# A decoder layer on one core: the relative bias written from the weights' queue, and a last norm that ends in columns

## The chip, the cores and the metric

The kernel runs on one NeuronCore of one Trainium2 chip. The metric is device time in microseconds (us) of one execution. TensorE is called PE in the profile, VectorE DVE, ScalarE ACT, GpSimd POOL and SyncE SP. SP and ACT each have a queue of DMA transfers of their own.

## The reference, cut to what matters

One layer: attention with a relative bias on 256 tokens of width 1024, a norm, a mixture of 32 experts of which each token takes 4, and a second norm. With 256 tokens there is one block of keys, so attention is plain causal attention.

```python
qkv = x @ w_in                                  # (256, 1024) @ (1024, 3072)
s = q k^T * Dh**-0.5 + rel_bias[t5_bucket(qpos - kpos)]   # causal, softmax, 8 heads
t = softmax(s) v @ w_out
h = layer_norm(ALPHA * x + t, ln_g[0], ln_b[0])
logits = h @ w_router + b_router                # top 4 of 32, softmax over the 4
for each chosen expert e:                       # clamped SwiGLU
    a = h @ w_gu[e] + b_gu[e];  g, u = split(a)
    f += gate * ((min(g,7) * sigmoid(1.702 g) * (clip(u,-7,7) + 1)) @ w_dn[e] + b_dn[e])
out = layer_norm(ALPHA * h + f, ln_g[1], ln_b[1])
```

## The kernel before

Everything is written out in one fixed order for each engine. Weights stream from HBM through 13 slots of 16 KB per partition (2 MB each). `fetch` takes the next slot's transfer from the list `todo`; its argument is the number of pieces, not of slots. `prefetch` issues as many as there are free slots. All weights go through the queue of SP, in the order of `todo`: six blocks of `w_in`, two slots of `w_out`, then for each expert four slots of `w_gu` and two of `w_dn`. The last expert's `w_dn` comes in another layout (`w_dl`), as four transfers of 1 MB.

**Start (L243 to L285).** SP loads the transposed input `xT` and the first block of weights (called w0 below) in pieces: four of 256 KB (L252), then two of 512 KB (L142), then the second block (w1) in two of 1 MB. ACT's queue loads the 32x8 table of the relative bias and a one-hot matrix. PE warms up on ones (L259) and multiplies the two (L269); DVE copies the product to `rrow` (L270). ACT's queue then writes `rrow` to a small DRAM tile `rd` in two transfers (L279, L280: 127 rows, then 256 rows, of 32 bytes each), and SP's queue reads it back as one overlapping pattern into `BT_rows` (L281), which must wait for both writes. Only behind that does SP issue the third block (`fetch(2)` at L282).

**Projection.** Inputs and weights are split into a high and a low part: ACT rounds the high part (`act_copy`, CAST in the profile at L180), DVE subtracts (L169 for weights, L276 for `xT`). PE then makes three products for each 128 rows of depth (L313 to L315), 96 products of 256 columns for each block of 512 columns of q and k. The block is evacuated at L323. The bias `BT` is first read by the softmax of head 0 (L362), which is issued together with the sixth of the twelve half-blocks.

**Experts.** Two experts share a gather and a scatter. `stage1` (L672) multiplies by `w_gu`, `swiglu` follows, `stage2` (L700) multiplies by `w_dn`. The loop ends with the first product of expert 30; behind it stand, in this order on PE: the transposes of its activation, a scatter, `spread_gain` (16 matmuls against the identity that copy gain and shift of the last norm to all partitions, evacuated by ACT into `gb2`), `stage1` of expert 31, `stage2` of expert 30 in two halves (one per slot of `w_dn`), and `stage2_columns` for expert 31 by column blocks (0, 1), (2) and (3), each followed by `add_columns`, which adds to `acc` and takes the norm's statistics.

**Last norm (`second_norm`).** For each of the two row tiles: aggregate (L197), square root on ACT (L198), reciprocal and one Newton step (L204 to L207), all on 128x1. The lower 512 columns are then normalized, scaled and shifted on DVE with two operations of 512 columns (L977, L978); the upper 512 are normalized on ACT (L984), scaled on POOL (L985) and shifted on DVE (L989). Four transfers of 256 KB write rows of the output. A branch follows, over further blocks for experts with more than 64 tokens; in the profiled execution it is not taken.

Of the kernel before, what the change touches and what calls it, by code (L numbers as in the profile page):

```python
# [11 lines left out]
F32 = mybir.dt.float32  # L12
# [4 lines left out]
AF = mybir.ActivationFunctionType  # L17
OP = mybir.AluOpType
# [4 lines left out]
S, D, H, DH = 256, 1024, 8, 128  # L23
NE, TOPK = 32, 4
KT = D // 128
# [3 lines left out]
EPS = 1e-5  # L29
# [31 lines left out]
def tile_decoder_layer(ctx: ExitStack, tc, a, out):  # L61
    nc = tc.nc
# [6 lines left out]
    def bank(name):  # L69
        return pm.tile([128, 512], F32, name=name)  # L70
# [5 lines left out]
    def tp_tile():  # L76
        return bank(next(three))
# [4 lines left out]
    def small(name, w, p=128, dt=F32):  # L82
        return cst.tile([p, w], dt, name=name)

    c = small("c", C_W)
# [5 lines left out]
    eps = small("eps", 1)  # L91
    ident = c[:, C_ID:C_ID + 128]
# [3 lines left out]
    gbT = c[:, C_LN:C_LN + 4 * KT]  # L96
# [5 lines left out]
    def slot(name, dt=F32):  # L102
        used[0] += 1
        assert used[0] <= W_SLOTS
        return wp.tile([128, SLOT], dt, name=name, tag="w")
# [8 lines left out]
    def source(key):  # L114
        kind, e, k = key
        if kind == "in":
            return a["w_in"][e]
        if kind == "dl":
            return a["w_dl"][k]
        return a["w_out"][k] if kind == "out" else a["w_gu" if kind == "gu" else "w_dn"][e, k]  # L120
# [10 lines left out]
    def fetch(pieces=1):  # L131
        key = todo.pop()
        src = source(key)
        t = slot("w").rearrange("p (k c) -> p k c", k=src.shape[1])
        load(t, src, pieces)
        w_tiles[key] = t

    def load(t, src, pieces):
        k = src.shape[1]
        for i in range(pieces):  # L140
            ks = slice(i * k // pieces, (i + 1) * k // pieces)
            nc.sync.dma_start(t[:, ks], src[:, ks])  # L142

    def prefetch():
        while todo and W_SLOTS - used[0] > reserve[0]:
            fetch(2 if todo[-1][0] == "dl" else 1)
# [38 lines left out]
    class Stats:  # L185
# [23 lines left out]
        def normal(self, r, engine):  # L209
            for s in HALVES:  # L210
                engine.tensor_scalar(r[:, s], r[:, s], self.mean, self.rstd, op0=OP.subtract, op1=OP.mult)
# [12 lines left out]
    x, acc = (t.rearrange("p (t d) -> p t d", t=2) for t in (BT, xT))  # L224
# [5 lines left out]
    BT_rows, BT = BT, BT.rearrange("p (s h) -> p s h", h=H)  # L230
# [4 lines left out]
    rrow = hp.tile([128, 3, H], F32, name="rrow")  # L235
# [28 lines left out]
    def rel_rows(row, ap):  # L264
        return bass.AP(tensor=rd.tensor, offset=rd.offset + row * H, ap=ap)
# [3 lines left out]
        nc.tensor.matmul(pr[:, i * H:(i + 1) * H], oh[:, i * 128:(i + 1) * 128], rb, start=True, stop=True)  # L269
    nc.vector.tensor_copy(rrow[:, :2], pr[:, :2 * H].rearrange("p (i h) -> p i h", i=2))  # L270
    fetch(2)

    def split_x(s):
        xhf, xlf = (t.rearrange("p k s -> p (k s)") for t in (xh, xl))
        act_copy(xhf[:, s], xT[:, s])
        nc.vector.tensor_tensor(xlf[:, s], xT[:, s], xhf[:, s].bitcast(F32), op=OP.subtract)  # L276

    split_x(slice(0, 256))
    nc.scalar.dma_start(rel_rows(0, [[H, 127], [1, H]]), rrow[:127, 2])  # L279
    nc.scalar.dma_start(rel_rows(127, [[H, 128], [128 * H, 2], [1, H]]), rrow[:, :2])  # L280
    nc.sync.dma_start(BT_rows, rel_rows(0, [[H, 128], [1, S * H]]))  # L281
    fetch(2)  # L282
    split(("in", ORDER[0], 0), act_copy, 4, lambda i: split_x(slice(256 << i, 512 << i)) if i < 2 else None)
    split_x(slice(1024, 2048))
    split(("in", ORDER[0], 1), act_copy, 4)  # L285
# [111 lines left out]
    for n in range(12):  # L397
        blk, i = ORDER[n // 2], n % 2
        last = n == 11
        if not last:  # L400
            split_next(("in", blk, i))
        if n == 1:
            nc.sync.dma_start(c, a["consts"])
            nc.sync.dma_start(router.rearrange("p k e -> p (k e)"), a["router"])
            reserve[0] = 1
            prefetch()
        for hh in score_at.get(n - 1, []):
            softmax(hh)
        if last:
            for hh in score_at.get(n - 1, []):  # L410
                softmax_norm(hh)
            split_next(("in", blk, i))
        (proj_qk if blk < 4 else proj_v)(blk, i)
        if i == 1:
            evac(blk, QT if blk < 2 else KTt)
        if not last:
            for hh in score_at.get(n - 1, []):
                softmax_norm(hh)
        for hh in score_at.get(n, []):
            scores(hh)  # L420
        for hh in trans_at.get(n, []):
            p_transpose(hh)
# [11 lines left out]
    stats = [Stats(hp, f"a{t}", 2 + t) for t in range(2)]  # L434
# [205 lines left out]
    mp = ctx.enter_context(tc.tile_pool(name="mp", bufs=1, reuse_waits="tile"))  # L640
# [104 lines left out]
    def spread(ps, cols, i, stop=True):  # L745

        for k in range(4):
            l = gbT[:, cols + 4 * i + k:cols + 4 * i + k + 1].to_broadcast([128, 128])
            nc.tensor.matmul(ps[:, k * 128:(k + 1) * 128], l, ident, start=True, stop=stop)
# [36 lines left out]
        nc.vector.tensor_copy(n_i, om[:, 95:96])  # L786
        nc.vector.tensor_tensor(om, om, fl, op=OP.mult)

    def spread_gain():

        for i in range(4):
            ps = tp_tile()
            spread(ps, 2 * KT, i)
            nc.scalar.copy(gb2[:, i * 512:(i + 1) * 512], ps)

    def more_blocks():

        bufs = itertools.cycle([slot("lw") for _ in range(2)])
# [125 lines left out]


    tail = slot("tail")
    gb2, aT_even = tail[:, :2 * D], tail[:, 2 * D:2 * D + 512].rearrange("p (j s c) -> p j s c", j=4, s=2)
    act_T(act, aT_even)
    pair_scatter(GT, Y, 1, False, (1,))
    GT = pair_slots_T(Gd)  # L930
    spread_gain()
    e = NE - 1
    hgu = stage1_bias(sel[:, e:e + 1].to_broadcast([3 * NE, CAP]))
    stage1(lambda k: xg[:, k, CAP:], lambda k: take(("gu", e, k)), hgu, lambda k: done(("gu", e, k)))
# [11 lines left out]
    stats = [Stats(mp, f"b{t}", 6) for t in range(2)]  # L946
# [20 lines left out]
    add_columns((2,), ("tp2", "yp"))  # L967
    stage2_columns(aT, (3,), ("hg", "hu"))
    add_columns((3,), ("o0", "o1"))
    g2, b2 = gb2[:, :D], gb2[:, D:]  # L970
    lo, hi = HALVES
    y = slot("y")[:, :2 * D].rearrange("p (t d) -> p t d", t=2)

    def scaled(st, t):

        d = y[:, t, lo]
        nc.vector.scalar_tensor_tensor(d, acc[:, t, lo], st.mean, g2[:, lo], op0=OP.subtract, op1=OP.mult)  # L977
        nc.vector.scalar_tensor_tensor(d, d, st.rstd, b2[:, lo], op0=OP.mult, op1=OP.add)  # L978
        nc.sync.dma_start(out[t * 128:(t + 1) * 128, lo], d)

    def normal(st, t):
        d = y[:, t, hi]
        nc.vector.scalar_tensor_tensor(st.v, st.mean, -1.0, st.rstd, op0=OP.mult, op1=OP.mult)
        nc.scalar.activation(d, acc[:, t, hi], AF.Identity, scale=st.rstd, bias=st.v)  # L984
        nc.gpsimd.tensor_tensor(d, d, g2[:, hi], op=OP.mult)  # L985

    def shifted(t):
        d = y[:, t, hi]
        nc.vector.tensor_tensor(d, d, b2[:, hi], op=OP.add)  # L989
        nc.sync.dma_start(out[t * 128:(t + 1) * 128, hi], d)  # L990

    def second_norm(stats):
        for st in stats:
            st.root()
        for t in range(2):
            stats[t].finish()
            normal(stats[t], t)
        for t in range(2):
            scaled(stats[t], t)
        for t in range(2):  # L1000
            shifted(t)

    second_norm(stats)
    more_blocks()
# [41 lines left out]
```

## Time and profile before

| | |
|---|---|
| median of 3 runs | 1062.68 us (1062.18 to 1062.95) |
| the profiled execution | 1062.37 us |
| its span, first to last instruction | 1060.5 us |
| PE busy | 972.7 us, 92% of the span |
| DVE, ACT, POOL busy | 272.9, 178.2, 7.3 us |
| read from HBM | 423.91 MB, 401 GB/s over the span |

The profiled execution's own time is 1.9 us longer than its span. A busy PE is not a PE at its peak: matmuls overlap and their ends are modelled. What bounds a stage is read from the chain of waits and from stretches of time. The granted clock of PE is 1.00 at the upper of its two levels (2.4 GHz) and 0.50 at the lower (1.2 GHz).

### The profile page before, as it was taken

Reading aid. Unit: us, or ns where it says so; the run is one execution under the profiler, and the core shown is the slowest. Engines: PE = TensorE matmul, PEld = TensorE weight load, DVE = VectorE, ACT = ScalarE, POOL = GpSimd, SP = SyncE. Lnnn points to the kernel's source line nnn. Section 1 sums busy time; section 2 is a strip of 40 time slices with the busy share of each in tenths; the row PEclk is TensorE's granted clock in tenths of the full one; section 3 lists DMA queues with packets and bytes.
Section 4 is the critical chain, followed back from the end, with each engine's and each line's share of the span. In section 5 each row is a group of like instructions: output and inputs, shape, how many; then the busy total and the mean of one; then the engine's idle time right before and its main releaser. Section 6 shows DMA issues by size and latency. Waiting matters only on the chain.

```text
span 1060.5 us, 11683 instructions
## 1 busy us (share of the span) xinstructions
PE 972.7 (92%) x5004; PEld 457.1 (43%) x5004; DVE 272.9 (26%) x571; ACT 178.2 (17%) x343; POOL 7.3 (1%) x8
## 2 busy tenths in 40 slices
PE   5999999999999999888888899999988898888893
PEld 5998753343434343333323353434323333333343
DVE  3467641212121212121111232221111212121115
ACT  3356241010101110101001010101001010101121
POOL 0000100000000000000000000000000000000001
PEclk7999999999999999999999989999999999999997
DMA  8993979999999999999999999999999999999991
GB/s 301 430 394 132 345 323 428 426 431 425 426 430 427 428 427 427 428 426 429 427 427 429 411 427 426 428 428 427 428 428 426 429 427 426 429 428 426 429 405 64
DMA packets 32551, 425.77 MB, mean 401 GB/s; under 512 B 4048, under 2 KB 4464, under 8 KB 6288
## 3 DMA queue, kind: packets, MB, share of 16 engines
q1 hardware_dynamic: 31728, 423.89, 95.0%
q10 hardware_dynamic: 768, 1.09, 0.3%
q8 instruction: 41, 0.67, 0.3%
q14 instruction: 14, 0.11, 0.0%
HBM read 423.91 MB, written 1.06 MB: 401 GB/s over the span
## 4 chain that ended last, share of the span: by engine, by line
DMA 60%; PE 34%; DVE 4%; ACT 2%; SPq 0%; issue 0%; DVEq 0%; ACTq 0%
DMA w<-in_w_gu 44%; DMA w<-in_w_dn 15%; PE yp L700 7%; PE hg L672 6%; PE hu L672 6%; PE tp L658 1%; PE o L742 1%; DMA w<-in_w_in 1%; PE tp L742 1%; PE tp L315 1%; PE tp L314 1%; PE tp L313 1%; PE o L313 1%; PE o L315 1%; PE o L314 1%; PE hg L715 0%
## 5 line engine op out<-in xcount | busy, mean ns | idle before, releaser
L672 PE MATMUL hg<-w,QT_KTt 128*64 128x512 f32 x960 | 249.8, 597 | 54.4 <-DMA w<-in_w_gu 54.4
L672 PE MATMUL hu<-w,QT_KTt 128*64 128x512 f32 x960 | 247.7, 592 | 0.0
L700 PE MATMUL yp<-w,QT_KTt 128*64 128x512 f32 x960 | 214.3, 599 | 0.7 <-ACT QT_KTt L690 0.7
L679 DVE TENSOR_SCALAR QT_KTt<-hg 128x512 f32<-128x512 f32 x32 | 22.1, 691 | 650.7 <-PE hg L672 650.7
L672 PEld LDWEIGHTS hg<-w,QT_KTt 128*64 128x64 f32 x960 | 65.9, 136 | 193.5 <-issue 125.9
L672 PEld LDWEIGHTS hu<-w,QT_KTt 128*64 128x64 f32 x960 | 70.8, 137 | 135.2 <-issue 135.2
L700 PEld LDWEIGHTS yp<-w,QT_KTt 128*64 128x64 f32 x960 | 66.6, 137 | 134.6 <-issue 121.2
L680 ACT ACTIVATE QT_KTt<-QT_KTt 128x512 f32<-128x512 f32 x32 | 20.1, 629 | 470.4 <-DVE QT_KTt L679 470.4
L704 ACT COPY QT_KTt<-yp 64x512 f32<-64x512 f32 x62 | 35.9, 579 | 224.4 <-PE yp L700 224.0
L658 PEld LDWEIGHTS tp<-OH,BT_xT 128*128 128x128 f32 x480 | 58.9, 200 | 12.0 <-issue 11.2
L658 PE MATMUL tp<-OH,BT_xT 128*128 128x128 f32 x480 | 63.2, 288 | 0.0
L169 DVE TENSOR_TENSOR whl<-w,whl 128x1024 fp32r<-128x1024 f32 (+1 forms) x36 | 38.1, 1102 | 27.1 <-ACT whl L180 27.1
L180 ACT CAST whl<-w 128x1024 fp32r<-128x1024 f32 (+1 forms) x36 | 32.5, 955 | 21.2 <-DMA w<-in_w_in 10.7
L564 DVE TENSOR_SCALAR QT_KTt<-tp,c 128x128 f32<-128x128 f32 x60 | 20.5, 403 | 44.4 <-PE tp L658 44.4
L742 PE MATMUL tp<-QT_KTt 128*128 128x512 f32 x60 | 30.7, 593 | 0.0
L742 PE MATMUL o<-QT_KTt 128*128 128x512 f32 x60 | 29.8, 618 | 0.0
L566 ACT ACTIVATE QT_KTt<-tp,c 128x128 f32<-128x128 f32 x60 | 22.5, 456 | 36.4 <-PE tp L658 36.4
L690 ACT COPY QT_KTt<-tp 128x512 f32<-128x512 f32 x31 | 18.6, 601 | 40.8 <-PE tp L689 36.5
L313 PE MATMUL o<-xhl,whl 128*128 128x256 f32 x48 | 14.9, 311 | 9.7 <-ACT whl L180 9.7
L681 DVE TENSOR_SCALAR hu<-hu 128x512 f32<-128x512 f32 x32 | 22.4, 699 | 3.0 <-PE hu L672 0.2
L683 DVE SCALAR_TENSOR_TENSOR QT_KTt<-hu,QT_KTt 128x512 f32<-128x512 f32 x32 | 22.1, 691 | 1.1
L682 DVE TENSOR_TENSOR QT_KTt<-QT_KTt 128x512 f32<-128x512 f32 x32 | 21.9, 684 | 0.1
(278 smaller groups left out, 785.1 us busy)
## 6 DMA issues: line engine op xcount, KB each, us to landing
w<-in_w_gu SPq DMA_DIRECT2D x128, 2048.0 KB, 39.1
w<-in_w_dn SPq DMA_DIRECT2D x62, 2048.0 KB, 39.1
w<-in_w_in SPq DMA_DIRECT2D x3, 2048.0 KB, 21.3
w<-in_w_in SPq DMA_DIRECT2D x4, 1024.0 KB, 9.3
w<-in_w_out SPq DMA_DIRECT2D x2, 2048.0 KB, 28.3
w<-in_w_dl SPq DMA_DIRECT2D x4, 1024.0 KB, 31.8
w<-in_w_in SPq DMA_DIRECT2D x4, 256.0 KB, 5.0
w<-in_w_in SPq DMA_DIRECT2D x2, 512.0 KB, 7.5
```

The source lines that it names most:

```text
L169: nc.vector.tensor_tensor(lo[:, s], w[:, s], hi[:, s].bitcast(F32), op=OP.subtract)
L180: nc.scalar.copy(o, i)
L313: nc.tensor.matmul(o, wh[:, k, js], xh[:, kk, :], start=kk == 0, stop=False)
L566: nc.scalar.activation(o, i, AF.Identity, scale=g, bias=b)
L658: nc.tensor.matmul(ps[:, k * 128:(k + 1) * 128], h[:, t, kk * 128:(kk + 1) * 128], OH[:, t].rearrange("p s c -> p (s c)"), start=t == 0, s ...
L672: nc.tensor.matmul(hgu[i][s * 64:(s + 1) * 64], xg(k), w[:, kk, q * 512:(q + 1) * 512], start=False, stop=k == KT - 1)
L679: nc.vector.tensor_scalar(g7, hgu[0], LIMIT, None, op0=OP.min)
L681: nc.vector.tensor_scalar(u7, u7, LIMIT, -LIMIT, op0=OP.min, op1=OP.max)
L683: nc.vector.scalar_tensor_tensor(sg, u7, 1.0, g7, op0=OP.add, op1=OP.mult)
L700: nc.tensor.matmul(y_ps[s], aT[:, kk % 4, kk // 4, :], w[:, k, HALVES[s ^ swap]], start=kk == 0, stop=kk == KT - 1)
L704: nc.scalar.copy(Y[s * 64:(s + 1) * 64, s ^ swap, :], y_ps[s])
L742: nc.tensor.matmul(po, GT[:, cb, t, :], Y[:, cb, :], start=True, stop=True)
```

## The change

Two parts that have nothing to do with each other.

At the start, the two writes of `rrow` move from ACT's queue to SP's, between the second and the third block of weights. The readback moves further back on SP, behind the fourth block.

At the end, `spread_gain` goes. Both row tiles share their roots (operations on 128x2). ACT normalizes the lower and DVE the upper 512 columns of each tile into `z`, PE transposes the 16 blocks of 128x128 into four PSUM banks, ACT and DVE apply scale and shift, which are now one number per partition, while they copy each 128x256 block out of PSUM, and four transfers write the output as columns (128 x 8 x 256); the host puts the axes back. `z` lies where `gb2` lay; `yT` takes the slot of `y`.

```diff
     fetch(2)
+    nc.sync.dma_start(rel_rows(0, [[H, 127], [1, H]]), rrow[:127, 2])
+    nc.sync.dma_start(rel_rows(127, [[H, 128], [128 * H, 2], [1, H]]), rrow[:, :2])
+    fetch(2)
 ...
     split_x(slice(0, 256))
-    nc.scalar.dma_start(rel_rows(0, [[H, 127], [1, H]]), rrow[:127, 2])
-    nc.scalar.dma_start(rel_rows(127, [[H, 128], [128 * H, 2], [1, H]]), rrow[:, :2])
-    nc.sync.dma_start(BT_rows, rel_rows(0, [[H, 128], [1, S * H]]))
-    fetch(2)
 ...
         if n == 1:
             nc.sync.dma_start(c, a["consts"])
             nc.sync.dma_start(router.rearrange("p k e -> p (k e)"), a["router"])
+            fetch()
+            nc.sync.dma_start(BT_rows, rel_rows(0, [[H, 128], [1, S * H]]))
 ...
-    def spread_gain():
-
-        for i in range(4):
-            ps = tp_tile()
-            spread(ps, 2 * KT, i)
-            nc.scalar.copy(gb2[:, i * 512:(i + 1) * 512], ps)
 ...
-    spread_gain()
 ...
     def second_norm(stats):
-        for st in stats:
-            st.root()
-        for t in range(2):
-            stats[t].finish()
-            normal(stats[t], t)
-        for t in range(2):
-            scaled(stats[t], t)
-        for t in range(2):
-            shifted(t)
+        u, rstd, nm, v = (r2[:, i] for i in range(4))
+        for t, st in enumerate(stats):
+            nc.vector.bn_aggr(st.t[:, 0:2], st.st.rearrange("p a b -> p (a b)"))
+            nc.scalar.activation(rstd[:, t:t + 1], st.var, AF.Sqrt, bias=eps)
+            nc.vector.tensor_scalar(v[:, t:t + 1], st.var, EPS, None, op0=OP.add)
+        nc.vector.reciprocal(rstd, rstd)
+        nc.vector.tensor_tensor(u, rstd, rstd, op=OP.mult)
+        nc.vector.tensor_tensor(u, u, v, op=OP.mult)
+        nc.vector.tensor_scalar(u, u, -0.5, 1.5, op0=OP.mult, op1=OP.add)
+        nc.vector.tensor_tensor(rstd, rstd, u, op=OP.mult)
+        for t, st in enumerate(stats):
+            nc.vector.scalar_tensor_tensor(nm[:, t:t + 1], st.mean, -1.0, rstd[:, t:t + 1], op0=OP.mult, op1=OP.mult)
+        for t, st in enumerate(stats):
+            nc.scalar.activation(z[:, t, lo], acc[:, t, lo], AF.Identity, scale=rstd[:, t:t + 1], bias=nm[:, t:t + 1])
+            nc.vector.tensor_scalar(z[:, t, hi], acc[:, t, hi], st.mean, rstd[:, t:t + 1],
+                                    op0=OP.subtract, op1=OP.mult)
+        names = ("tp0", "tp1", "tp2", "yp")
+        ps = [bank(n).rearrange("p (k s) -> p k s", k=2) for n in names]
+        for t in range(2):
+            for k in (0, 4, 1, 5, 2, 6, 3, 7):
+                nc.tensor.transpose(ps[k // 2][:, k % 2, t * 128:(t + 1) * 128], z[:, t, k * 128:(k + 1) * 128], ident)
+        for i in range(2):
+            for k in (2 * i, 2 * i + 4, 2 * i + 1, 2 * i + 5):
+                o, p = yT[:, k], ps[k // 2][:, k % 2]
+                g, b = gbT[:, 2 * KT + k:2 * KT + k + 1], gbT[:, 3 * KT + k:3 * KT + k + 1]
+                if k < 4:
+                    nc.scalar.activation(o, p, AF.Identity, scale=g, bias=b)
+                else:
+                    nc.vector.tensor_scalar(o, p, g, b, op0=OP.mult, op1=OP.add)
+            for k in (2 * i, 2 * i + 4):
+                nc.sync.dma_start(out[:, k:k + 2], yT[:, k:k + 2])
```

How the instructions stand on the engines at the two places: first ACT at the start of the program, before (`whl` is the split weight, `xhl` the split input, `rd` the DRAM tile).

```order
L180 CAST xhl<-BT_xT 128x256
L279 DMA rd<-rrow 127x8
L280 DMA rd<-rrow 128x2x8
L180 CAST whl<-w 128x512
L180 CAST xhl<-BT_xT 128x256
```

And ACT at the same place now:

```order
L180 CAST xhl<-BT_xT 128x256
L180 CAST whl<-w 128x512
L180 CAST xhl<-BT_xT 128x256
L180 CAST whl<-w 128x512
L180 CAST xhl<-BT_xT 128x512
```

The two writes no longer stand ahead of the first cast of a weight. On SP, before, from the second half of w0 on:

```order
L142 DMA w<-in_w_in 128x1024 x2
L142 DMA w<-in_w_in 128x2048 x2
L281 DMA BT_xT<-rd 128x2048
L142 DMA w<-in_w_in 128x2048 x2
L403 DMA c<-in_consts 128x452
L404 DMA router<-in_router 128x288
L142 DMA w<-in_w_in 128x4096 x3
```

And on SP now:

```order
L142 DMA w<-in_w_in 128x1024 x2
L142 DMA w<-in_w_in 128x2048 x2
L272 DMA rd<-rrow 127x8
L273 DMA rd<-rrow 128x2x8
L142 DMA w<-in_w_in 128x2048 x2
L402 DMA c<-in_consts 128x452
L403 DMA router<-in_router 128x288
L142 DMA w<-in_w_in 128x4096
L405 DMA BT_xT<-rd 128x2048
L142 DMA w<-in_w_in 128x4096 x2
```

The writes stand ahead of the third block, and the readback, which waits for them, moved from ahead of the third block to behind the fourth.

## Rows read from the trace of the kernel before

**Rows 1.** The page: shares of the span in the chain that ended last, by line.

```profile
DMA w<-in_w_gu 44%; DMA w<-in_w_dn 15%; PE yp L700 7%; PE hg L672 6%; PE hu L672 6%; PE tp L658 1%; PE o L742 1%; DMA w<-in_w_in 1%; PE tp L742 1%; PE tp L315 1%; PE tp L314 1%; PE tp L313 1%; PE o L313 1%; PE o L315 1%; PE o L314 1%; PE hg L715 0%
```

**Rows 2.** Stretches: us, busy of PE, PEld, DVE, ACT, POOL, clock, DMA share, GB/s.

```profile
16.00:20.00 4.00, 4.00 (x20) 4.00 (x20) 4.00 (x7) 4.00 (x8) 0.00 (x0) 0.50 0.28 79
...
100.00:104.00 4.00, 4.00 (x22) 3.40 (x21) 3.08 (x5) 3.56 (x4) 0.00 (x0) 1.00 0.00 0
...
148.00:152.00 4.00, 4.00 (x20) 1.15 (x16) 2.86 (x3) 1.07 (x1) 0.00 (x0) 1.00 1.05 451
...
1050.00:1055.00 5.00, 0.00 (x0) 0.00 (x0) 4.93 (x5) 0.47 (x1) 2.52 (x2) 0.50 0.14 54
```

**Rows 3.** Timeline of the start: start, duration, instruction, idle time before and its releaser.

```profile
5.65 0.42 DVE L276 TENSOR_TENSOR xhl<-BT_xT,xhl 128x256 fp32r<-128x256 f32 x1
...
6.97 7.58 ACTq L280 DMA_DIRECT2D rd<-rrow  x1
14.59 0.62 ACT L180 CAST whl<-w 128x512 fp32r<-128x512 f32 x1 [10.71 <-DMA w<-in_w_in]
...
15.26 0.58 PE L313 MATMUL o<-xhl,whl 128*128 128x256 f32 x1 [9.74 <-ACT whl L180]
...
21.49 0.35 PE L313 MATMUL o<-xhl,whl 128*128 128x256 f32 x1
...
29.82 0.28 PE L313 MATMUL hg<-xhl,whl 128*128 128x256 f32 x1
```

**Rows 4.** First block's pieces: issues on SP, and their time from issue to landing.

```profile
1.19 0.42 SPq L252 DMA_DIRECT2D w<-in_w_in  x1
...
DMA to landing us min/median/max: 3.2/5.0/5.4
...
4.51 1.46 SPq L142 DMA_DIRECT2D w<-in_w_in  x2
...
w<-in_w_in SPq DMA_DIRECT2D x1, 512.0 KB, 8.0
```

**Rows 5.** ACT's DMA queue in 6.2 to 16 and 16 to 19 us; the readback's issue.

```profile
q10 hardware_dynamic: 22, 0.00, 0.1%
...
q10 hardware_dynamic: 378, 0.01, 7.1%
...
18.73 0.33 SPq L281 DMA_DIRECT2D BT_xT<-rd  x1
```

**Rows 6.** Timeline: first casts of the third block, first use of the bias.

```profile
33.76 2.00 ACT L180 CAST whl<-w 128x1024 fp32r<-128x1024 f32 x2 [1.48 <-DVE whl L169]
...
50.66 0.94 DVE L362 SCALAR_TENSOR_TENSOR p<-hg,BT_xT 128x128 f32<-128x128 f32 x2
```

**Rows 7.** Tail: two pieces of the chain; the last `w_dn` slot, issue and landing.

```profile
1006.88 3.57 PE tp L749 x32
...
1028.76 3.58 PE yp L700 x16
...
988.86 0.33 SPq L142 DMA_DIRECT2D w<-in_w_dn  x1
...
w<-in_w_dn SPq DMA_DIRECT2D x1, 2048.0 KB, 39.1
```

**Rows 8.** Timeline of the last norm, and a scaled copy of 128 columns (page).

```profile
1046.80 0.30 DVE L197 BATCH_NORM_AGGREGATE rs_b<-st_b 128x2 f32<-128x36 f32 x1
1047.14 0.71 ACT L198 ACTIVATE rs_b<-rs_b,eps 128x1 f32<-128x1 f32 x2 [2.93 <-DVE rs_b L197]
...
1048.25 0.21 DVE L207 TENSOR_SCALAR rs_b<-rs_b 128x1 f32<-128x1 f32 x1
...
1048.69 1.77 ACT L984 ACTIVATE y<-BT_xT,rs_b 128x512 f32<-128x512 f32 x2 [0.85 <-DVE rs_b L983]
...
1055.15 0.94 SPq L990 DMA_DIRECT2D out<-y  x2
...
L566 ACT ACTIVATE QT_KTt<-tp,c 128x128 f32<-128x128 f32 x60 | 22.5, 456 | 36.4 <-PE tp L658 36.4
```

More of the change, by code (lines that the diff above doesn't have):

```diff
@@ L926, in tile_decoder_layer @@
     tail = slot("tail")
-    gb2, aT_even = tail[:, :2 * D], tail[:, 2 * D:2 * D + 512].rearrange("p (j s c) -> p j s c", j=4, s=2)
+    y, aT_even = tail[:, :2 * D], tail[:, 2 * D:2 * D + 512].rearrange("p (j s c) -> p j s c", j=4, s=2)
     act_T(act, aT_even)
@@ L969, in tile_decoder_layer @@
     add_columns((3,), ("o0", "o1"))
-    g2, b2 = gb2[:, :D], gb2[:, D:]
     lo, hi = HALVES
[L972 to L990, printed above, removed]
-    def second_norm(stats):
-        for st in stats:
-            st.root()
-        for t in range(2):
-            stats[t].finish()
-            normal(stats[t], t)
-        for t in range(2):
-            scaled(stats[t], t)
-        for t in range(2):
-            shifted(t)
+    z, yT = y.rearrange("p (t d) -> p t d", t=2), slot("yT")[:, :2 * D].rearrange("p (k s) -> p k s", k=KT)
@@ new lines, in tile_decoder_layer @@
+    r2 = mp.tile([128, 4, 2], F32, name="r2")
+    def second_norm(stats):
+        u, rstd, nm, v = (r2[:, i] for i in range(4))
[16 more added lines that the diff above has]
+        ps = [bank(n).rearrange("p (k s) -> p k s", k=2) for n in names]
+        for t in range(2):
+            for k in (0, 4, 1, 5, 2, 6, 3, 7):
[10 more added lines that the diff above has]
+                nc.sync.dma_start(out[:, k:k + 2], yT[:, k:k + 2])
@@ L1040 @@
            for k, v in arrays.items()}
-    out = nc.dram_tensor("out_0", (S, D), F32, kind="ExternalOutput").ap()
+    out = nc.dram_tensor("out_0", (128, KT, S), F32, kind="ExternalOutput").ap()
     with tile.TileContext(nc) as tc:
@@ L1044 @@
     res = run_bass_kernel_spmd(nc, [arrays], core_ids=[0])
-    return res.results[0]["out_0"].reshape(1, S, D)
+    return np.ascontiguousarray(res.results[0]["out_0"].reshape(128, KT, S).transpose(2, 1, 0)).reshape(1, S, D)
```

## The prediction

> **What bounds the kernel now.** I read the page first. The chain that ended last is 59% transfers of expert weights [rows 1], so for most of the span the kernel waits for HBM. That doesn't mean that only bytes count. The next view is the table of stretches [rows 2]: from about 148 us on the transfers run at the rate of the whole rest (451 GB/s in 148 to 152 us), but before that they stop, to 79 GB/s in 16 to 20 us and to 0 in 100 to 104 us. In these gaps the slots are full and SP waits until compute frees one. So the moment at which the saturated stretch begins is set by the chain of compute ahead of it, and whatever moves that chain moves the end of the program by the same amount, as long as the gap at 100 us and its neighbours leave room to take it from. The other place that counts is what follows the last weights.
>
> The timeline of the start [rows 3] shows where the chain of compute begins. ACT casts the first piece of weights only at 14.59 us, and PE starts on it at 15.26 after 9.74 us of idleness. The profile puts ACT's wait down to the piece's transfer. The landings contradict that [rows 4]: the first piece was issued at 1.19 us and the quickest of the four took 3.2 us, so it lies there at about 4.4, and the last of the four at 8.5 at the latest. What ends at 14.55 is the issue of the second write of `rrow`, which stands ahead of the cast on ACT and took 7.58 us. After 15.26 PE is busy without a break (4.00 of 4.00 us in 16 to 20), at first at half its clock: the clock rises at 21.49 and the block ends at 29.82 [rows 3]. From there to the experts it is never idle for long, so this start shifts everything behind it.
>
> **The start, step by step.** With both writes gone from ACT, its first weight cast runs from 4.4 to 5.0 us. PE must first finish the two small products for the bias, whose copy and the input's low half on DVE follow; DVE's row for the low half is at 5.65 and takes 0.42 [rows 3], which puts the end of PE's own products at about 5.5. PE's first real product thus starts at 5.5 and not at 15.26: 9.8 us earlier. Three bounds on that. The first product that uses the weight's low half waits for DVE: 5.65 + 0.42 for the input and about 0.7 for the weight make 6.8; it was about 0.7 behind the first product before, so this shift is at least 9.2. On the other side, before, PE ran 6.2 us at half clock (15.26 to 21.49). If the clock rises sooner after the start, up to half of the 6.2 us is won on top, 3.1, so 12.9 at most; and the data then binds: the second piece of 512 KB was issued at about 4.5 and landed 8.0 later, 12.5 [rows 4], behind which two casts of 0.62, a subtraction of 0.7 and 12 products at 0.12 remain, 15.9 us, which is early enough. If the clock rises as late as before, relative to the first product, the shift is the 9.8 itself. I take 9.8, as nearest to the rows.
>
> What SP now does instead. The two writes go into the queue behind w1, whose transfer ends at about 16.5 us as before (in 16 to 20 us only 79 GB/s are left) [rows 2]. What the writes cost there the trace doesn't show, but it bounds it. On ACT's queue hardly anything of them moved while weights were under way (22 packets up to 16 us), and 378 of the 400 went in 16 to 19 us, all before the readback's issue at 18.73 [rows 5]. Their packets took 7.1% of 16 engines in 3 us, 3.4 us of one engine, 0.009 us a packet; at the other end, if all engines worked evenly through the 2.7 us, 0.11 us a packet. The third block's first half, 1 MB or 2.4 us, then lands at 16.5 + 2.7 + 2.4 = 21.6, plus up to 1 for the landing. It is cast at 33.76 before [rows 6], so 24.0 now, and PE needs it only when the second block is done, 29.82 + 96 x 0.12 - 9.8 = 31.5, less 2.0 for its casts: 29.5. There are some 7 us of cover. The readback stands behind the fourth block: 21.6 + 2.4 + 0.9 for the constants + 4.8 + 2.4 is 32, and the bias is first read at 50.66 - 9.8 = 40.9. Both cost nothing; if the cover of 7 us went, each further us would cost one. In exchange SP no longer stands still until 18.73.
>
> A rule of the Trainium skill speaks against just this. Its page "DMA: Bandwidth & Descriptors", section "Why a DMA increments its semaphore by 16 and not by 1", says that a transfer over 127 partitions runs on a single one of the 16 engines, and "Queues, rings and completion order" says that an engine takes its descriptors in ring order. By that, the first write puts 127 of its rows ahead of every following weight on one engine. With 0.009 us each that is 1.3 us and the sum is unchanged; with 0.11 us each the price is that of the second rival below. The first of the two sections can't be checked here, since no row tells engines apart.
>
> **The tail, step by step.** `spread_gain` took 3.57 us on PE's chain [rows 7]. Its removal isn't worth that much, for PE then runs into the weights. The last slot of `w_dn` was issued at 988.86 and landed 39.1 later, at 1027.96, and the products that read it start at 1028.76 [rows 7]. So PE can come forward by some 0.7 us there and then waits; less a small delay of the release I take 0.6. The bounds are 0.3 (as long a delay as 0.5) and the full 3.57, if the last transfers get ahead of compute.
>
> The last norm: DVE aggregates from 1046.80, the first square root starts at 1047.14 and ACT's first wide operation at 1048.69 [rows 8]. Now the roots are joint: the second one ends at 1047.85, and six small operations at about 0.2 (one of them is in the rows: 0.21) bring the first wide operation to 1049.05, 0.35 later. ACT takes 0.89 for each tile (1.77 for two), so the first tile is ready at 1049.95 and the second at 1050.85; DVE's halves run beside it. Then 16 transposes: at the lower clock, to which PE has fallen by then (0.50 in 1050 to 1055 us) [rows 2], twice the 0.11 us that a pass of 128 columns costs in `spread_gain` (3.57 for 32 passes) make 3.5 us, 1049.95 to 1053.5, with the first pair of blocks complete after nine of them, 1052.0. ACT's four copies of 256 columns come at about 0.5 each (a scaled copy of 128 takes 0.456) and end at 1054.0, DVE's beside them; SP issues the last two transfers by 1054.75. Before, SP's last issue ended at 1055.15 + 0.94 = 1056.09. The last norm comes out 1.3 us shorter, provided that what follows the last issue (4.4 us to the end of the span) stays. Bounds: a transpose may cost two passes, 3.5 us more, less what ACT's copies hide then, which makes the norm 1.5 longer; at full clock 1.0 more is saved, 2.3 in all.
>
> **The sum**, against the profiled execution's 1062.37: 9.8 + 0.6 + 1.3 = 11.7, so 1050.7; the median of the runs is 0.3 above that execution, so 1051.0.
>
> **The rivals.**
>
> 1. *The start does not move.* The profile is right and the cast waited for its weights, so the writes were in nobody's way. For it: the releaser in the row. Against it: landings of at most 5.4 us. Only the tail's 1.9 remains: 1060.8.
>
> 2. *One late engine.* The 127 rows go one after another at 0.11 us, 14 us, and all following weights wait for that engine: the third block's first half lands at 16.5 + 14 + 2.4 + 1 = 33.9, 4.4 after the need. For it: small writes did wait on ACT's queue. Against it: the engine time of their packets is a twelfth of that. 1055.4.
>
> 3. *The weights' queue is held, the other sign.* SP is stopped by the writes as ACT was, and for longer, because here the whole stream stands behind them. What decides is when the third block lands: behind 29.5 every us is lost, and behind 41.2 the 11.7 are used up. ACT's hold of 7.58 us from 7 us on, even once for each write, ends at 22 and is still covered. A hold to 45 would give 1066. Nothing in the rows reaches that far.
>
> 4. *The clock rises early, or the tail wins whole.* Start 12 instead of 9.8, or `spread_gain` 3.57, or both: 1045.5 to 1048.5. For it: PE has been busy since the warm-up when the first product comes; against it: it was also busy before and began at half clock.
>
> **How the numbers follow.** My forecast (1048.5 to 1053.5) has 0.63; rival 4 has 0.15; rival 2 and smaller losses of its kind, 1053.5 to 1060, 0.13; rival 1, 0.05; rival 3, 0.04. The range of 8 in 10 takes the forecast, most of rival 4 and the near part of rival 2: 1047.0 to 1055.0. A measurement of this kernel can tell about 0.2% (2.1 us) from no change: faster 0.91, same 0.05, slower 0.04.
>
> **What would show it.** In the profile of the changed kernel the first weight cast should stand at about 4.4 us and PE's first product at 5.5, the end of the first block near 20 and the first stretch without transfers near 100 shorter by about 10. The saturated stretch should begin about 10 us earlier. In the tail PE should wait for a slot of `w_dn` or `w_dl`. From the last aggregate to SP's last issue should be 8.0 us instead of 9.3. A third block cast later than it is needed, or a first product behind 8 us, would prove me wrong.

## The result, and the profile after

The changed kernel takes 1053.47 us (median of 4 runs, 1052.76 to 1054.74), the kernel before 1062.78 in the same series (4 runs, 1062.18 to 1062.95): ratio 0.9915, 95% interval 0.9898 to 0.9932. The forecast of 1051.0 was 2.5 too low; the time lies inside the range. The profiled execution took 1053.08 us, its span is 1051.3 (before 1060.5), so 9.2 us went.

The chain of the page, in the kernel after, beside [rows 1]:

```profile
DMA w<-in_w_gu 37%; DMA w<-in_w_dn 15%; PE yp L701 9%; PE hg L673 8%; PE hu L673 8%; PE tp L659 2%; PE o L743 1%; PE tp L743 1%; PE tp L314 1%; PE tp L313 1%; PE tp L312 1%; PE o L314 1%; PE o L312 1%; PE o L313 1%; PE tp L690 1%; DVE whl L169 1%
```

Transfers fell from 59% to 52% of it. The timeline of the start, after (columns as in [rows 3]):

```profile
4.92 0.62 ACT L180 CAST whl<-w 128x512 fp32r<-128x512 f32 x1 [1.05 <-DMA w<-in_w_in]
5.71 0.38 PE L312 MATMUL o<-xhl,whl 128*128 128x256 f32 x1
7.16 0.30 SPq L272 DMA_DIRECT2D rd<-rrow  x1
7.20 0.28 PE L312 MATMUL o<-xhl,whl 128*128 128x256 f32 x1
7.74 9.46 SPq L273 DMA_DIRECT2D rd<-rrow  x1
17.25 1.08 SPq L142 DMA_DIRECT2D w<-in_w_in  x2
18.40 0.28 PE L312 MATMUL hg<-xhl,whl 128*128 128x256 f32 x1
22.92 2.00 ACT L180 CAST whl<-w 128x1024 fp32r<-128x1024 f32 x2 [2.05 <-DMA w<-in_w_in]
```

PE's first product stands at 5.71 instead of 15.26, 9.55 earlier, and the first block ends at 18.40 instead of 29.82 [rows 3], 11.4 earlier: the products are short (0.28) from 7.20 on, 1.5 us after the first one, where before they became so only after 6.2 us. The hold has moved along with the writes: 7.58 us on ACT's queue became 9.46 on SP's, and the third block is issued only at 17.25. Its first cast waits for it until 22.92. PE needs that block 96 products of 0.12 behind the first block's end, at 29.9, so the cast has until 27.9: 5 us of cover are left.

Stretches after (columns as in [rows 2]):

```profile
16.00:20.00 4.00, 4.00 (x36) 4.00 (x35) 3.07 (x5) 2.93 (x6) 0.00 (x0) 1.00 0.53 134
88.00:92.00 4.00, 4.00 (x22) 3.37 (x21) 3.02 (x5) 3.66 (x5) 0.00 (x0) 1.00 0.00 0
116.00:120.00 4.00, 4.00 (x19) 1.61 (x18) 3.03 (x18) 0.85 (x2) 1.11 (x1) 0.71 1.00 414
120.00:124.00 4.00, 4.00 (x13) 2.09 (x12) 0.22 (x2) 0.67 (x1) 0.00 (x0) 0.50 0.98 416
124.00:128.00 4.00, 4.00 (x33) 3.73 (x33) 0.26 (x1) 0.39 (x2) 0.00 (x0) 0.93 0.38 160
1040.00:1045.00 5.00, 3.67 (x16) 3.27 (x16) 2.21 (x6) 2.64 (x5) 0.00 (x0) 0.50 0.09 34
```

The stretch without transfers at 100 us, which I had forecast to be shorter, has moved instead: 0 GB/s now stand at 88 to 92 us, so there too later weights start only when compute frees slots. New to the eye is 116 to 124 us, the routing stage (the choice of the experts and the first gather): PE's granted clock is 0.71 and then 0.50. The stretches of the same stage before:

```profile
128.00:132.00 4.00, 4.00 (x17) 1.37 (x17) 2.48 (x15) 1.46 (x2) 0.51 (x1) 0.85 0.98 412
132.00:136.00 4.00, 4.00 (x24) 3.55 (x23) 0.48 (x2) 0.06 (x1) 0.00 (x0) 0.72 1.04 442
```

And its timeline before, the first tile's choice of experts (`M`) and the first product with expert weights:

```profile
128.19 0.19 DVE L521 TENSOR_TENSOR M<-lg,rest 128x32 f32<-128x32 f32 x1
...
138.14 1.08 PE L672 MATMUL hg<-w,BT_xT 128*64 128x512 f32 x4
```

The timeline after, with four 512-column products of the first bias between the two:

```profile
116.80 0.19 DVE L522 TENSOR_TENSOR M<-lg,rest 128x32 f32<-128x32 f32 x1
117.38 1.69 PE L573 MATMUL hg<-QT_KTt,c 32*64 32x512 f32 x4
128.40 1.08 PE L673 MATMUL hg<-w,BT_xT 128*64 128x512 f32 x4
```

`M` comes 11.4 us earlier and the first expert product only 9.7: 1.65 us are lost between the two. A further 0.5 goes until expert 30's last wait for `w_gu`. Its row before:

```profile
998.72 1.08 PE L672 MATMUL hg<-w,QT_KTt 128*64 128x512 f32 x4 [1.24 <-DMA w<-in_w_gu]
```

And the same row after:

```profile
989.49 1.08 PE L673 MATMUL hg<-w,QT_KTt 128*64 128x512 f32 x4 [1.24 <-DMA w<-in_w_gu]
```

The tail after, from the timeline: PE's last waits for weights, then the last norm:

```profile
1013.96 3.65 PE L701 MATMUL yp<-w,tail 128*64 128x512 f32 x16 [1.32 <-DMA w<-in_w_dn]
1018.75 3.65 PE L701 MATMUL yp<-w,tail 128*64 128x512 f32 x16 [0.56 <-DMA w<-in_w_dn]
1036.86 0.30 DVE L971 BATCH_NORM_AGGREGATE rs_b<-st_b 128x2 f32<-128x36 f32 x1
1039.18 1.52 ACT L982 ACTIVATE tail<-BT_xT,r 128x512 f32<-128x512 f32 x2 [1.28 <-DVE r L980]
1040.05 1.33 PE L989 MATMUL tp<-c,tail 128*128 128x128 f32 x5 [4.49 <-ACT tail L982]
1042.70 1.93 ACT L995 ACTIVATE yT<-tp,c 128x256 f32<-128x256 f32 x4 [1.99 <-PE tp L989]
1043.74 1.81 SPq L999 DMA_DIRECT2D out<-yT  x4
```

And from the view of line 999 after, the time from issue to landing of its four output transfers:

```profile
DMA to landing us min/median/max: 2.2/3.6/4.5
```

PE waits for both slots of `w_dn`, as forecast. The first aggregate stands 9.94 us earlier than in [rows 8]. SP's last issue ends at 1045.55, 8.69 behind the aggregate (before 9.29), but from there to the end of the span it is 5.75 us instead of 4.4, since the last transfer lands 4.5 us behind its issue. From the aggregate to the end the norm takes 14.44 us; before, 13.70. Other runs repeat both: with the old norm it is 13.66 to 13.71 (e1, e4, e9), with the new one unchanged 14.18 to 14.51 (e2, e3, e5, e7, e12).

### The profile page after: what moved, and what is told of

It reads as the page before. It is cut to its first block, busy times and chain, and to the rows that moved or that the text cites. A ratio compares the mean times of both kernels' runs of the same rounds, so it can differ in the third digit from the quotient of the medians.

```text
span 1051.3 us, 11647 instructions
## 1 busy us (share of the span) xinstructions
PE 973.3 (93%) x4988; PEld 453.5 (43%) x4988; DVE 269.7 (26%) x568; ACT 178.4 (17%) x343; POOL 4.3 (0%) x6
## 4 chain that ended last, share of the span: by engine, by line
DMA 52%; PE 41%; DVE 4%; ACT 2%; issue 0%; DVEq 0%; SPq 0%; ACTq 0%
DMA w<-in_w_gu 37%; DMA w<-in_w_dn 15%; PE yp L701 9%; PE hg L673 8%; PE hu L673 8%; PE tp L659 2%; PE o L743 1%; PE tp L743 1%; PE tp L314 1%; PE tp L313 1%; PE tp L312 1%; PE o L314 1%; PE o L312 1%; PE o L313 1%; PE tp L690 1%; DVE whl L169 1%
## 5 line engine op out<-in xcount | busy, mean ns | idle before, releaser
L659 PEld LDWEIGHTS tp<-OH,BT_xT 128*128 128x128 f32 x480 | 58.6, 199 | 11.4 <-issue 10.6
L690 PE MATMUL tp<-c,QT_KTt 128*128 128x128 f32 x128 | 19.3, 274 | 2.2 <-DVE QT_KTt L684 2.2
```

The lines of the kernel that those rows point to most:

```text
L659: nc.tensor.matmul(ps[:, k * 128:(k + 1) * 128], h[:, t, kk * 128:(kk + 1) * 128], OH[:, t].rearrange("p s c -> p (s c)"), start=t == 0, s ...
L690: nc.tensor.transpose(ps[:, j * 128:(j + 1) * 128], act[:, j * 128:(j + 1) * 128], ident)
```

## The experiments

All ratios are against the kernel before, run on the same chip. "Start" is the part of the change that moves the writes, "tail" the rest. "Warm" says that products whose result nobody reads are to keep PE at its upper clock there.

| run | what it is | median, us (range, runs) | ratio (95%) |
|---|---|---|---|
| e1 | before + start | 1049.67 (1049.25 to 1054.38, 5) | 0.9884 (0.9866 to 0.9902) |
| e2 | before + tail | 1062.75 (1061.92 to 1064.16, 11) | 0.9998 (0.9989 to 1.0007) |
| e3 | after, output in blocks | 1053.14 (1049.56 to 1054.01, 5) | 0.9902 (0.9887 to 0.9918) |
| e4 | before, first write of 128 rows | 1056.28 (1055.40 to 1056.55, 5) | 0.9936 (0.9923 to 0.9950) |
| e5 | after, first write of 128 rows | 1053.51 (1049.75 to 1054.56, 4) | 0.9911 (0.9896 to 0.9927) |
| e12 | after, three writes of 127 rows | 1050.22 (1049.86 to 1052.99, 4) | 0.9880 (0.9864 to 0.9897) |
| e7 | after, warm routing | 1049.86 (1049.42 to 1053.96, 5) | 0.9882 (0.9866 to 0.9899) |
| e11 | before, warm routing | 1059.66 (1059.03 to 1061.14, 6) | 0.9967 (0.9955 to 0.9979) |
| e9 | before + start, warm routing | 1050.05 (1049.90 to 1051.17, 4) | 0.9878 (0.9863 to 0.9893) |
| e6 | after, warm transposes | 1052.27 (1050.97 to 1053.53, 4) | 0.9898 (0.9883 to 0.9914) |
| e8 | after, transposes in pairs | 1053.29 (1051.84 to 1054.34, 4) | 0.9903 (0.9888 to 0.9919) |
| e10 | e5, e6, e7 and e8 together | 1049.20 (1048.17 to 1053.38, 5) | 0.9879 (0.9862 to 0.9897) |

**e1 and e2: which part carries the gain.** e1 is the changed kernel with `spread_gain` and the last norm of before; e2 is the changed kernel with the order of the start of before (shown are the lines that come back):

```diff
 ...
+    nc.scalar.dma_start(rel_rows(0, [[H, 127], [1, H]]), rrow[:127, 2])
+    nc.scalar.dma_start(rel_rows(127, [[H, 128], [128 * H, 2], [1, H]]), rrow[:, :2])
+    nc.sync.dma_start(BT_rows, rel_rows(0, [[H, 128], [1, S * H]]))
+    fetch(2)
```

> The kernel before with the start of the changed one alone (writes on SP's queue, readback behind the fourth block; old last norm and spread_gain). Theory A, from the trace after: the start alone carries the gain, so about 9 us faster than before (1053 to 1055), with the first block's end near 18.4 us, and the tail adds nothing. Rival B, the prediction's sum: 9.8 from the start and a further 1.9 from the tail, so this kernel stands 1 to 2 us above the changed one.

> The changed kernel with the start of the kernel before (writes on ACT's queue): the new last norm and no spread_gain alone. Theory A: 0.7 from spread_gain and 0.6 from the norm's compute are given back by a last transfer that lands 1.4 later after its issue, so within 1 us of before. Rival B, the prediction's sum: 1.9 faster than before, about 1060.9.

The tail alone is worth nothing that the runs resolve (0.9998, within 0.1%), so the start carries the gain. e1's median even lies 3.8 us below that of the changed kernel. Its runs say why that is not to be taken at its word: three lie at 1049.25 to 1049.67, two at 1052.34 and 1054.38. What the two groups are, e5 and e7 tell.

**e3: the layout of the output.** Each of the four transfers writes one block of 256 KB instead of 128 rows 8 KB apart:

```diff
-                nc.sync.dma_start(out[:, k:k + 2], yT[:, k:k + 2])
+                nc.sync.dma_start(out[k // 2].rearrange("p (k s) -> p k s", k=2), yT[:, k:k + 2])
```

> The changed kernel, but each of the four output transfers writes one contiguous block of 256 KB of the output tensor, instead of 2 KB pieces that stand 8 KB apart; the host's permutation of axes changes with it. If the late landing of the last transfer (4.5 us after its issue, against 3.1 before) comes from the 8 KB pitch, it falls to about 3 and the kernel gets 1.3 faster than the changed one. If it comes from the four transfers being issued close together, or from something else on the transfer engines, it stays at 4.4 and the time with it.

The landings are 2.4, 3.3 and 4.5 us (shortest, median, longest) and the time is the same. The layout isn't what makes the last landing late.

**e4 and e5: 128 rows instead of 127.** In the kernel before (e4, on ACT's queue) and after (e5, on SP's), the DRAM tile gets a row more and the readback starts one row later:

```diff
-    rd = dr.tile([383, H], F32, name="rd")
+    rd = dr.tile([384, H], F32, name="rd")
 ...
-    nc.sync.dma_start(rel_rows(0, [[H, 127], [1, H]]), rrow[:127, 2])
-    nc.sync.dma_start(rel_rows(127, [[H, 128], [128 * H, 2], [1, H]]), rrow[:, :2])
+    nc.sync.dma_start(rel_rows(0, [[H, 128], [1, H]]), rrow[:, 2])
+    nc.sync.dma_start(rel_rows(128, [[H, 128], [128 * H, 2], [1, H]]), rrow[:, :2])
 ...
-            nc.sync.dma_start(BT_rows, rel_rows(0, [[H, 128], [1, S * H]]))
+            nc.sync.dma_start(BT_rows, rel_rows(1, [[H, 128], [1, S * H]]))
```

> The kernel before, with one thing changed: the first write of the bias goes over 128 partitions instead of 127 (the DRAM tile has one row more in front, the readback begins one row later). The writes stay on ACT's queue. Theory: the 7.58 us of the second write's issue come from the first write's 127 rows on one engine; then the issue takes under 1 us, the first weight cast stands near 7.4 us instead of 14.59 and the kernel is 5 to 8 us faster than before. Rival: small writes on ACT's queue wait for the weights whatever their spread; then the issue still takes 7 us or more and nothing changes.

> The changed kernel with the first write over 128 rows instead of 127 (the small DRAM tile has one row more). Theory (the hold only moved to SP, and there it is covered): the second write's issue on SP takes less than 1 us instead of 9.46, the third block is issued near 9 us instead of 17.25, the stretch 16 to 20 us no longer runs at 134 GB/s; PE's first product stays at 5.7 and the first block's end at 18.4, and the time stays at 1053.5 within 1 us. Rival (the stream of weights is delayed by the hold and that costs time somewhere): the time falls by 2 us or more and the saturated stretch begins before 135.5.

The timeline of e4's start:

```profile
5.99 0.36 ACTq L279 DMA_DIRECT2D rd<-rrow  x1
7.19 0.39 ACTq L280 DMA_DIRECT2D rd<-rrow  x1
7.62 0.62 ACT L180 CAST whl<-w 128x512 fp32r<-128x512 f32 x1 [3.79 <-DMA w<-in_w_in]
```

And the timeline of e5's:

```profile
8.17 0.38 SPq L273 DMA_DIRECT2D rd<-rrow  x1
8.77 1.60 SPq L142 DMA_DIRECT2D w<-in_w_in  x2
```

One row more in the *first* write takes the *second* one's issue from 7.58 to 0.39 us on ACT and from 9.46 to 0.38 on SP. So it was the write of 127 rows that held the queue. The edit also moves the second write's target by one row, but that can't be the cause: in e12 the issue that is held for 8.41 us goes to row 0 of a tile of its own. The rule that the prediction drew from the Trainium skill ("DMA: Bandwidth & Descriptors", "Why a DMA increments its semaphore by 16 and not by 1": 127 partitions put everything on one engine) agrees with that, though no row tells engines apart. For the kernel before, the row alone brings 6.7 us (1062.96 in the same series to 1056.28). After, it brings nothing (1053.51 against 1053.47), although the third block is issued 8.5 us earlier: the hold lies under its cover. For the gain there are thus two ways, to move the writes or to widen the first one; the first brings more here, since in e4 the first cast still stands at 7.62, behind both issues, and not at 4.92.

**e12: how long the hold grows.**

```diff
+    more = [dr.tile([127, H], F32, name=f"more{i}") for i in range(2)]
 ...
     nc.sync.dma_start(rel_rows(0, [[H, 127], [1, H]]), rrow[:127, 2])
+    for m in more:
+        nc.sync.dma_start(m, rrow[:127, 2])
```

> The changed kernel with two more writes of 127 rows behind the first one, to DRAM tiles that nobody reads. In the changed kernel the third block is issued at 17.25 us, its first cast waits for it until 22.92, and PE needs it 11.5 us behind the first block's end at 18.4, which is 29.9, or 27.9 at the cast. Theory (each write of 127 rows holds the weights' queue for some 9 us, and the hold costs nothing until its cover of 5 us is gone): SP is held until 34 to 36 us, the third block is cast at 40 to 42, PE stands still or waits for 12 to 14 us behind the second block, the saturated stretch begins 10 to 14 us later than 135.5, and the time is 1063 to 1067. If more such writes hold the queue no longer than one does, SP goes on near 17 to 18, and the time stays at 1053 within 1.5 us. If the hold grows but the weights have room to come in before the experts, the first products of the third block are late and the time is not.

The timeline of SP in e12:

```profile
8.22 9.16 SPq L275 DMA_DIRECT2D more<-rrow  x2
17.48 1.42 SPq L276 DMA_DIRECT2D rd<-rrow  x1
18.94 0.94 SPq L142 DMA_DIRECT2D w<-in_w_in  x2
```

My theory fell in its second half: the hold doesn't add up by writes. Of the two issues in the first row the first alone takes 8.41 us, to 16.63; the second takes 0.71 and the write behind it 1.42, and the third block is issued 1.7 us later than in the changed kernel. The end of the hold stays at 16.0 to 17.2 us in all the profiled kernels with such a write on SP, about where the second block's transfers run out (428 GB/s in 12 to 16 us, 134 in 16 to 20). That suggests that the queue goes on once what stands ahead of the narrow write has moved, but on ACT's queue, before, the hold ended at 14.55, when the weights were still moving (426 GB/s in 12 to 16 us). What ends the hold stays open. The point from which a longer hold would cost was thus not reached, and the cover of 5 us wasn't tried to its end.

**e7, e11 and e9: the clock in the routing stage.** Two filler products move in among the 32-column products of the router, and two are added:

```diff
 ...
-    logits(1)
+    for k in range(KT):
+        logits(1, (k,))
+        if k % 2:
+            filler(1, "tp0")
 ...
-    filler(2)
```

e7 does this to the kernel after, e11 to the kernel before, e9 to e1.

> The changed kernel with the two filler products ahead of the first positions moved into the second tile's 32-column router products, and two more of them there (one after every second of eight). PE comes to the positions 0.4 us later by that. Theory (the 6.9 us at half clock in 116 to 128 us cost 3.4 us, and whether PE falls to half clock there is what makes the times two-valued, near 1049.5 and near 1053): the clock stays above 0.9 in 116 to 124, from the first tile's M to the first product of the experts it takes about 8.5 us instead of 11.4, and the runs lie near 1050. Rival (what PE does ahead of the stretch has no part in the fall): the clock falls as before, the time is the same or 0.4 longer, with runs at 1053 to 1054.

> The kernel before with nothing but the filler products of the routing stage moved. Theory (in the kernel before PE also runs at half clock for about 3.4 us in 128 to 136 us, which costs 1.7 us, of which the two more products take 0.4): the clock stays at 1.00 there, the time is 1061.2 to 1061.8. Rival (the fall costs nothing before, since the transfers bind there): 1062.8 or 0.4 more.

> The new start with the tail of before, and the filler products of the routing stage moved as in the run with the warm routing. Against that run (1049.86) only the tail differs. Theory (the old tail costs 0.7 us more at spread_gain and 0.7 to 0.8 less behind the first aggregate, so the two tails are worth the same): 1049 to 1050.5, at full clock in 116 to 128. Rival (the changed tail is dearer by itself, as the lower median of the start alone, 1049.67 against 1053.47, suggests): 1046 to 1048.

The stretches of the routing stage in e7:

```profile
116.00:120.00 4.00, 4.00 (x31) 3.08 (x32) 3.58 (x20) 1.04 (x4) 2.55 (x2) 1.00 0.92 324
120.00:124.00 4.00, 4.00 (x29) 2.81 (x26) 1.26 (x8) 1.52 (x2) 0.00 (x0) 1.00 1.04 436
```

Its timeline there, beside the changed kernel's rows of 117.38 and 128.40 us above:

```profile
118.24 0.19 DVE L522 TENSOR_TENSOR M<-lg,rest 128x32 f32<-128x32 f32 x1
118.84 1.07 PE L573 MATMUL hg<-QT_KTt,c 32*64 32x512 f32 x4
126.55 1.08 PE L675 MATMUL hg<-w,BT_xT 128*64 128x512 f32 x4
```

From `M` to the first expert product it takes 8.3 us at full clock, 11.6 in the changed kernel. (`M` itself stands 1.44 us later in e7, as the first block's end does, 19.83 against 18.40: see the clock at the start, below.) e5, which has no more filler than the changed kernel, was profiled in one of its quicker executions (1049.75; its other three took 1052.96 to 1054.56), and that one shows the full clock too, in its stretches:

```profile
116.00:120.00 4.00, 4.00 (x24) 2.02 (x24) 3.35 (x20) 0.75 (x2) 1.50 (x1) 1.00 0.92 377
120.00:124.00 4.00, 4.00 (x32) 3.38 (x30) 0.48 (x2) 1.06 (x2) 0.00 (x0) 1.00 1.01 428
```

The first expert product in e5's timeline:

```profile
125.48 1.08 PE L673 MATMUL hg<-w,BT_xT 128*64 128x512 f32 x4
```

From `M`, at 117.19 there, that is 8.3 us again. So most of the distance between the two groups of times is two courses of the clock in this stage, 3.3 us apart; no kernel was profiled in both. Of the profiled executions with the new start, those that fell to 0.50 in 120 to 124 (after, e1, e3, e6, e8, e12) took 1051.56 to 1053.70 us, those that didn't (e5, e7, e9, e10) 1049.20 to 1051.17. With the moved filler 12 of 14 runs (e7, e9, e10) lie below 1051.5, without it 8 of 26 (after, e1, e3, e5, e8, e12; e6, whose tail is shorter, is left out). The two slower runs with filler weren't profiled, so whether the clock fell in them is open. e12's low median is such a draw, not a gain, and so is e1's.

With the stage warm in both, e11 to e9 is the start alone: 1059.66 to 1050.05, 9.6 us. And e9 to e7 is the tail alone: 1050.05 to 1049.86, nothing beyond the spread of the runs. e11 itself gained 3.3 us where 1.2 to 1.8 were expected; its profiled execution shows 1.6 of it (8.3 us from `M` to the product instead of 9.95). That execution took 1060.89, 1.2 more than e11's median, so the rest lies in runs that were not traced.

**e6, e8 and e10: the last norm.** e6 puts 18 products that nobody reads ahead of the transposes; e8 transposes first, for both tiles, what the first two transfers need:

```diff
+        warm = bank("hg")
+        for i in range(18):
+            nc.tensor.matmul(warm[:64], sel[:, e:e + 1].to_broadcast([3 * NE, CAP]), bgu[:, :512],
+                             start=i == 0, stop=i == 17)
 ...
-        for t in range(2):
-            for k in (0, 4, 1, 5, 2, 6, 3, 7):
+        for t, ks in ((0, (0, 4, 1, 5)), (1, (0, 4, 1, 5)), (0, (2, 6, 3, 7)), (1, (2, 6, 3, 7))):
+            for k in ks:
```

> The changed kernel with 18 products of 512 columns, whose result nobody reads, in the 4.6 us in which PE waits between the last addition's products and the transposes of the last norm. Theory (the transposes cost 0.21 us each because PE's granted clock is 0.50 there after idling): they take 0.11 each, the sixteen end 1.5 us or more earlier, SP's last issue ends 0.8 to 1.4 us earlier relative to the first aggregate (8.69 now), and the granted clock in 1040 to 1045 is above 0.9. Rival (the time of a transpose is that of its weight load, whatever the clock): 0.21 each, nothing moves.

> The changed kernel with the sixteen transposes in another order: the eight blocks that the first two output transfers need first, for both row tiles, then the other eight. Theory (the last transfer lands 4.5 us after its issue because all four transfers, 1 MB, are issued within 1.8 us and take 2.9 us of the 16 DMA engines): the first two are issued about 0.9 us earlier, the last issue stays where it was, and its landing falls to 3.5 to 3.8 us; the span behind the first aggregate (14.44 us) is 0.7 to 0.9 shorter. Rival (the landing is long for the transfers' own sake, layout or a packet beside them): the last landing stays at 4.5 and the span behind the aggregate stays at 14.4.

> The changed kernel with the write over 128 rows, the filler in the routing stage, the 18 products ahead of the transposes and the transposes in the order of the transfers. If the effects add (1049.9 for the warm routing; 1.8 less behind the first aggregate for the warm transposes, 0.2 to 0.6 more for their order), the time is 1047.0 to 1048.2 and the span behind the first aggregate 12.0 to 12.5. If the transposes are no longer what the output waits for, the order brings nothing and the time is 1048.

The timeline of e6: the fillers, the first five transposes and the issues:

```profile
1035.81 4.07 PE L987 MATMUL hg<-bgu,sel 96*64 96x512 bf16 x18
1040.36 0.77 PE L993 MATMUL tp<-c,tail 128*128 128x128 f32 x5 [0.48 <-ACT tail L982]
1042.87 2.55 SPq L1003 DMA_DIRECT2D out<-yT  x4
```

Its stretch there:

```profile
1040.00:1045.00 5.00, 1.97 (x16) 1.73 (x16) 2.53 (x7) 2.95 (x6) 0.00 (x0) 1.00 0.18 60
```

And its output transfers, issue to landing:

```profile
DMA to landing us min/median/max: 2.6/3.0/3.2
```

The clock stays at 1.00, a transpose costs 0.11 instead of 0.21, and the span behind the aggregate falls from 14.44 to 12.62. SP's last issue came only 0.45 us earlier (8.24 behind the aggregate; I had expected 0.8 at least), because ACT's four copies of 0.48 bind then. The greater part comes behind it: the first transfer is issued 1.2 us earlier, and the longest landing is 3.2 us.

e8's landings, for its four output transfers:

```profile
DMA to landing us min/median/max: 2.2/2.6/3.9
```

At the same half clock the order alone brings the last landing to 3.9 and the span behind the aggregate to 13.68, 0.76 less. With the old tail, which issues in two pairs, the second pair lands in 3.1 (e9). Together with e3 this speaks for bunching as the cause of the late landing: with four transfers of 256 KB issued within 1.81 us the longest landing is 4.2 to 4.5 us in every profile (after, e2, e3, e5, e7, e12), with the issues spread over 2.3 to 2.6 us (e6, e8, e10) 3.2 to 3.9. The medians of e6 and e8 don't resolve such sizes, since the routing stage moves single runs by 3.3.

e10 has the lowest median of the study, 1049.20 us, by 4.3 below the changed kernel and by 13.8 below the one before. That is above the 1047.0 to 1048.2 that I had expected if the effects add, and its runs (1048.17 to 1053.38) don't separate it from e7. In its profile the span behind the aggregate is 12.63, as e6's. The order brings the last issue 0.43 us further forward (7.81 behind the aggregate), but the issues stand closer together and the longest landing is 3.8 instead of 3.2: once the transposes are warm, their order brings nothing more.

## Why the prediction came out as it did

The direction, the place and most of the size were right; the steps in order:

- **The cast waited for the writes, not for its weights.** Right: the cast went from 14.59 to 4.92, the first product from 15.26 to 5.71, 9.55 earlier against 9.8. Rival 1 is out. With the routing stage warm on both sides the start is worth 9.6 (e11 to e9).
- **The clock at the start.** I took no gain and kept 3.1 as a bound. The products reached their short duration 1.5 us after the first instead of 6.2, and the block's end came 11.4 earlier: 1.9 on top, which is the first half of rival 4. But that is a draw as well. With the same start, e7, e8, e9 and e10 took the longer products for 3.7 to 4.4 us, and their first block ended at 19.83 to 20.12 instead of 18.25 to 18.91 (after, e1, e3, e5, e6, e12); by those the shift is 9.7 to 10.0, the forecast's 9.8. e11, with the old start, took them for 4.9 us, so the 9.6 from e11 to e9 hold hardly anything of this draw. The timeline of e9 shows it:

```profile
6.15 0.58 PE L312 MATMUL o<-xhl,whl 128*128 128x256 f32 x1
10.52 0.28 PE L313 MATMUL o<-xhl,whl 128*128 128x256 f32 x1
20.12 0.28 PE L312 MATMUL hg<-xhl,whl 128*128 128x256 f32 x1
```

- **The weights' queue.** Rival 3's mechanism happened: SP was held for 9.46 us. Its price was worked out rightly as nothing: the third block was cast at 22.92 (forecast 24.0) with 5 us of cover, and taking the hold away (e5) changes nothing. My reading of how narrow writes are paid (0.009 or 0.11 us a packet) missed what they do, which is to hold the next issue. Two slips in the numbers there change nothing: 127 rows at 0.009 us are 1.1 us, not 1.3, and a hold of SP to 45 would, with the 3.4 us that I allowed from there to the landing, give some 1070 and not 1066.
- **The chain carries the shift to the end.** Not whole: 1.65 us were lost in the routing stage, where PE ran longer at half clock, and 0.5 more until the last wait for `w_gu` of expert 30 (998.72 before, 989.49 after). The first is shown by e7 and is not the start's doing: e2, with the start of before, took 11.6 us from `M` to the first expert product, the kernel before 9.95, e4 9.9. The cause of the second is open, and it is no larger than what the runs differ by anyway: from the first expert product to the end of the span after, e5, e7 and e12 take 922.2 to 922.9. The sum didn't have a term for the clock outside the two edited places.
- **`spread_gain`.** Forecast 0.6; the shift grows from 9.23 to 9.94, so 0.7. PE waits for `w_dn`, as said.
- **The last norm.** This is the step that failed: 1.3 gained in the sum, 0.74 lost in the profile. The last issue came 8.69 behind the aggregate instead of 8.0, for I had put in nothing for handing over from PE to ACT (the first copy starts at 1042.70, the ninth transpose at 1041.81). And the proviso that 4.4 us from the last issue to the end stay didn't hold: 5.75. The change issues in one bunch what before went out in two pairs, and by e3, e6, e8 and e10 that is the likely reason.

In sum 11.4 - 1.65 - 0.5 + 0.7 - 0.75 = 9.2. Of the 2.5 us by which the forecast was off, the norm makes 2.0 and the unexplained loss 0.5; the gain of 1.6 and the loss of 1.65 from the clock cancel each other, and that is luck, since neither was in the sum.

## What to carry to other kernels

A row that puts a wait down to a transfer is to be held against that transfer's own landing; here that one comparison carried the whole gain. A wait that is moved is moved, not removed: ask where its cover is on the new queue, and whether its cause can go instead (128 rows in place of 127 was 6.7 us for the kernel before). And where a stage ends in several transfers, count the bytes that are issued together: what follows the last issue is not a constant.

## What the hardware showed

- A write of 127 rows of 32 bytes lets its own issue pass in 0.30 to 0.47 us and holds the *next* DMA issue of the same engine for 7.4 to 9.5 us while weights are under way (ACT's queue in before, e2 and e11, SP's in the others); with 128 rows the next issue took 0.38 to 0.39 (e4, e5, e10). Two more such writes lengthened the wait for the third block by 1.7 us only.
- The runs of one kernel can lie 5 us apart (e1: 1049.25 to 1054.38). In the profiled executions 3.3 us of that go with whether PE's granted clock falls to 0.50 in a stage of 32-column products and waits that lasts 8 us, and 1 to 2 us with when PE's products become short at the start. Four products of 512 columns among those of the router, two of them new (0.4 us of PE's time), kept the clock at 1.00 there in every profiled execution.
- PE idle for 4.5 us between the last addition and the transposes came back at 0.50; 18 unused products in that gap kept 1.00, and cost nothing on the path.
